# Output projection of a hybrid attention layer: the last two groups of weights as 2 x 2 blocks with seven products, and a fixed order on DVE and ACT behind the last attention slot

## The chip, the cores and the metric

One Trainium2 chip, one of its cores. The metric is the device time of the whole kernel in microseconds (us). The engines are named as in the profile: PE is TensorE (matmuls; PEld are its weight loads), DVE is VectorE, ACT is ScalarE, POOL is GpSimd, SP is SyncE, which here only issues transfers. Each engine has a queue of its own and works through it in order.

## What is computed

A decoder layer of 512 tokens by 1024 channels in float32. A modulated RMSNorm and an input projection give queries, keys, values and gates for two groups of eight heads; group A does sliding-window attention, group B three branches of attention; each group's output is multiplied by a SiLU gate, and the two are joined and projected:

```python
y = jnp.concatenate([o_a.reshape(Bn, S, D_A) * jax.nn.silu(z_a.astype(jnp.float32)),
                     o_b.reshape(Bn, S, D_B) * jax.nn.silu(z_b.astype(jnp.float32))], axis=-1)
out = y.astype(x.dtype) @ w_out
return x + gate[:, None, :] * out
```

`w_out` is 1024 x 1024. This last product, with the gate and the sum behind it, is the part that the change touches.

## The kernel before

**Numbers as pairs.** Each float32 operand of a large matmul is kept as two tiles of type float32r: a high part, which ACT copies, and a low part, which DVE makes by subtracting the high part. A product takes three matmuls: high by high, high by low, low by high. For weights, `split` (from L166) does this for a piece of 128 x 512 elements: ACT at L176 writes `wh`, DVE at L177 writes `wl`. The pieces lie in a pool of four buffers each (`pw`); a fifth piece waits until the matmuls of the first are done. `split_to` (L182) calls `split` along a fixed list of weight groups up to a given piece plus `ahead` further ones. `load_next` (L150) issues the next raw weight load on SP (L158) when a raw buffer (`rawp`, five of them) is used up; two halves make one group.

**Layout of the output projection.** Everything is transposed: tokens lie along the free dimension. y consists of eight tiles of 128 channels x 512 tokens, `yh[c]` and `yl[c]`: c = 0 to 3 belong to group A, c = 4 to 7 to group B (r = c - 4). `make_y` (L805) forms y from the attention output and the gate (DVE, L808), its high part (ACT, L810) and its low part (DVE, L811). The weights come in four groups o0 to o3, each for 256 of the 1024 outputs. `unit_col` (L478) does one channel group of 128 outputs: eight steps k, each three matmuls (L484) of 128 x 128 weights by 512 columns, into one PSUM bank `pj`; `PJ` hands out three banks in turn. Behind it DVE computes gate times bank plus x (L1037, tile `fin`) and SP stores the result (L1038). x comes by a load on ACT's queue (L1025 for the first two channel groups, L1031 for the others). The eighth channel group is done in two halves of 256 tokens.

**Where the order comes from.** The attention is a row of slots (`run`): scores on PE, softmax on DVE and ACT, scaling on DVE (`slot_scale`, L907), transposes on PE copied by ACT (`slot_trans`, tile `ptT`, L923 and L933), and the products with V on PE (`slot_pv`, L949 and L955, bank `po`). Projection work is fed between the slots as a stream. The instructions are then placed on each engine's queue by a list scheduler of the programming framework, which takes what it holds to be ready and urgent; PE's instructions of the attention blocks are chained in the written order with `in_order` (L66) through `block` (L490), and the two early loads of x are placed with it on ACT's queue. Nothing chains DVE and ACT in the output projection. When the last slot's `slot_pv` is done, y7 is made straight from PSUM; y4 and y5 had been kept as plain attention outputs (`ob`, L964) because their gates weren't ready at their time, and are made at the end of the program too; y6 had been made earlier.

Of the kernel before, what the change touches and what calls it, by code (L numbers as in the profile page):

```python
# [9 lines left out]
F32 = mybir.dt.float32  # L10
# [4 lines left out]
OP = mybir.AluOpType  # L15
# [10 lines left out]
LINE = 640  # L26
GW = 280
AHEAD = 6
NT2 = 40
WAIT_L, WAIT_M = 4, (0, 8)  # L30
PER_A, PER_B = 3.6, (3.5, 1.6, 7)
NEAR = 256
# [32 lines left out]
@contextmanager  # L65
def in_order(tc, after=(), only=None):  # L66

    traced = tc.nc.cur_bb.bb.instructions
    n = len(traced)
    last = dict(after)  # L70
    yield last
    info = mybir.DependencyInfo(mybir.DependencyClass.NoSync, mybir.DependencyReason.DATA)
    for i in tc.nc.cur_bb.bb.instructions[n:]:
        if only and i.engine != only:
            continue
        if i.engine in last:
            tc.add_manual_dep(i, last[i.engine].name, info, reason="in_order")
        last[i.engine] = i
# [3 lines left out]
def hybrid_layer_kernel(ctx, tc, A, out):  # L82
# [67 lines left out]
    def load_next():  # L150
        if pending:
            g, h = pending.pop(0)
            t = rawp.tile([128, 4, GW], F32, name="raw")
            if g[:4] == "gate":
                raws[g, h] = t.rearrange("p a b -> p (a b)")[:, 0:D]
            else:
                raws[g, h] = t[:, :, 0:A["w_" + g].shape[3]]
            SP.dma_start(raws[g, h], A["w_" + g][h])  # L158

    COL = ("kv_cmp", "z_a0", "z_a1", "z_b0", "z_b1", "o0", "o1", "o2", "o3")  # L160
    split_list = [(g, p) for g in ("kv_cmp", "kv_sel", "kv_win_g", "q_b0", "q_b1", "z_a0", "z_a1", "z_b0", "z_b1",
                                   "o0", "o1", "o2", "o3") for p in range(4)]
    split_pos = {e: n for n, e in enumerate(split_list)}
    split_done = [0]

    def split(g, p):  # L166

        if g in COL:
            src = raws[g, p % 2][:, :, 128 * (p // 2):128 * (p // 2) + 128]
        else:  # L170
            src = raws[g, p // 2][:, 2 * (p % 2):2 * (p % 2) + 2, :]
        sh = [src.shape[1], src.shape[2]]
        view = lambda t: t[:, 0:sh[0] * sh[1]].rearrange("p (k n) -> p k n", k=sh[0])
        wh = view(pw.tile([128, 2 * GW], F32R, name="wh"))
        wl = view(pw.tile([128, 2 * GW], F32R, name="wl"))
        ACT.activation(wh, src, AF.Copy)  # L176
        DVE.tensor_tensor(wl, src, wh.bitcast(F32), op=OP.subtract)  # L177
        pieces[g, p] = (wh, wl)
        if p == 3 or (p == (2 if g in COL else 1)):
            load_next()  # L180

    def split_to(g, p, ahead):  # L182

        while split_done[0] < min(len(split_list), split_pos[g, p] + ahead + 1):
            n, q = split_list[split_done[0]]
            if not all((n, h) in raws for h in ((0, 1) if n in COL else (q // 2,))):
                break
            split(n, q)
            split_done[0] += 1
# [242 lines left out]
    def W2(name, shape=(128, 512)):  # L432
        return mp.tile(list(shape), F32, name=name, tag="w2", bufs=5)
# [41 lines left out]
                              start=k == 0 and m == 0, stop=k == 7 and m == 2)  # L475
                yield cost

    def unit_col(g, ch, bank, src=(hh, hl), tok=slice(0, S)):  # L478

        for k in range(8):  # L480
            split_to(g, 2 * ch + k // 4, AHEAD)
            wh, wl = (x[:, k % 4, :] for x in pieces[g, 2 * ch + k // 4])
            for m, (w, h) in enumerate(((wh, src[0][k]), (wh, src[1][k]), (wl, src[0][k]))):
                PE.matmul(bank, w, h[:, tok], start=k == 0 and m == 0, stop=k == 7 and m == 2)  # L484
            yield 0.65

    chain = {}
# [1 line left out]
    @contextmanager  # L489
    def block():  # L490

        with in_order(tc, chain, PE.engine) as last:
            yield
        chain.update(last)

# [304 lines left out]
        else:  # L800
            sz[n - 4] = z

    yh, yl = {}, {}

    def make_y(c, o, z):  # L805

        yf = W2("yf")
        DVE.scalar_tensor_tensor(yf, o, 0.5, z, op0=OP.mult, op1=OP.mult)  # L808
        yh[c], yl[c] = T2(F32R, f"yh{c}"), T2(F32R, f"yl{c}")
        ACT.activation(yh[c], yf, AF.Copy)  # L810
        DVE.tensor_tensor(yl[c], yf, yh[c].bitcast(F32), op=OP.subtract)  # L811

    def gen2():
        posts.append(cmp_attn())
# [122 lines left out]
    def slot_pv(sl):  # L937
        kind, r, br, i = sl["id"]
        if (kind, r) not in po:
            po[kind, r] = ps_o.tile([128, 512], F32, name="po")  # L940
        o = po[kind, r]
        v = (va, vs, vw, None)[br]
        nb, j0 = sl["w"] // 128, sl["lo"] // 128
        last = kind == "a"
        first_of = kind == "a" or br == 3
        for b in range(nb):
            for g in range(2):
                vb = (vs, vw)[b][:, 0] if br == 3 else v[:, j0 + b]
                PE.matmul(o[64 * g:64 * g + 64, 128 * i:128 * i + 128], vb[:, 64 * g:64 * g + 64],  # L949
                          sl["T"][g][:, b, :], start=first_of and b == 0, stop=last and b == nb - 1,  # L950
                          skip_group_check=True)
        if i == NB - 1 and br in (0, 2):
            if kind == "b":
                for e in range(2):
                    PE.matmul(o, vc[e].rearrange("p g d -> p (g d)"), PTc[r], start=False, stop=e == 1,  # L955
                              skip_group_check=True)
            if kind == "a":
                o_a[r] = T2(F32, f"oa{r}")
                ACT.activation(o_a[r], o, AF.Copy)
            elif r in sz:  # L960
                make_y(4 + r, o, sz[r])
            else:
                o_a["b", r] = T2(F32, f"ob{r}")
                ACT.activation(o_a["b", r], o, AF.Copy)  # L964

    late = {}

    def run(slots, stream):
        n = len(slots)
        group = []  # L970
        for t in range(n + 3):
            per = PER_A if t < 16 else PER_B[t - 16 >= PER_B[2]]
            if t < n:
                kind, r, br, i = slots[t]["id"]
                if kind == "a" and i == 0 and r >= 2:
                    load_bias_b(r - 2)
            if 0 <= t - 2 < n:
                with block():
                    slot_trans(slots[t - 2])
            if 0 <= t - 1 < n:  # L980
                slot_scale(slots[t - 1])
            if t < n:
                with block():
                    slot_scores(slots[t])
                if t == n - 12:
                    late[ACT.engine] = [i for i in tc.nc.cur_bb.bb.instructions if i.engine == ACT.engine][-1]
            stream.adv(per / 2)
            if 0 <= t - 3 < n:
                group.append(slots[t - 3])
                kind, r, br, i = slots[t - 3]["id"]  # L990
                if i == NB - 1:
                    with block():
                        for sl in group:
                            slot_pv(sl)
# [21 lines left out]
    for r in range(4):  # L1016
        if 4 + r not in yh:
            make_y(4 + r, o_a["b", r], sz[r])


    with in_order(tc, late, ACT.engine):
        xrs = []
        for n in range(2):
            xrs.append(mp.tile([128, S], F32, name="xr", tag="qc", bufs=2))
            ACT.dma_start(xrs[n], A["xT"][n])  # L1025
    for n in range(8):
        if n < 2:
            xr = xrs[n]
        else:
            xr = mp.tile([128, S], F32, name="xr", tag="qc", bufs=2)  # L1030
            ACT.dma_start(xr, A["xT"][n])  # L1031
        f = W2("fin")
        for tok in ((slice(0, S),) if n < 7 else (slice(0, 256), slice(256, S))):
            b = PJ()[:, tok]
            for _ in unit_col(f"o{n // 2}", n % 2, b, (yh, yl), tok):
                pass
            DVE.scalar_tensor_tensor(f[:, tok], b, gate[:, n:n + 1], xr[:, tok], op0=OP.mult, op1=OP.add)  # L1037
            SP.dma_start(out[n][:, tok], f[:, tok])  # L1038


def _layout(inp):
# [24 lines left out]
    rows = np.concatenate([pair(r) for r in range(4)] + [512 + pair(r) for r in range(4)])  # L1066
    wo = g("w_out")[0][rows].reshape(8, 128, 4, 256)
    for q in range(4):
        a[f"w_o{q}"] = halves(wo[:, :, q].transpose(1, 0, 2))
# [41 lines left out]
```

## Time and profile before

| | |
|---|---|
| three runs | 311.12, 312.45, 313.27 us; median 312.45 |
| profiled execution, its own time | 312.03 us |
| its span, first to last instruction | 309.4 us |
| mean granted TensorE clock | 0.999 |
| DVE busy over the span | 241.6 us (78%) |
| ACT busy over the span | 194.9 us (63%) |
| last matmul ends, last DVE instruction ends | 306.25, 306.76 us |

A span is counted from the first instruction of the core to its last, the landing of the last store included; the execution's own time is 2.6 us longer. Rows of groups give the line of the kernel, the engine, the operation with the tile that it writes and those that it reads, the shape, the count, then busy time and mean duration in ns, and the engine's idle time ahead of them. Rows of the timeline give start and length in us; a row with a count is a run of equal instructions, and its length goes from the first start to the last end. Instructions of one engine overlap a little, so the distance of two starts is shorter than a duration.

### The profile page before, as it was taken

Reading aid. Unit: us, or ns where it says so; the run is one execution under the profiler, and the core shown is the slowest. Engines: PE = TensorE matmul, PEld = TensorE weight load, DVE = VectorE, ACT = ScalarE, POOL = GpSimd, SP = SyncE. Lnnn points to the kernel's source line nnn. Section 1 sums busy time; section 2 is a strip of 40 time slices with the busy share of each in tenths; the row PEclk is TensorE's granted clock in tenths of the full one; section 3 lists DMA queues with packets and bytes.
Section 4 is the critical chain, followed back from the end, with each engine's and each line's share of the span. In section 5 each row is a group of like instructions: output and inputs, shape, how many; then the busy total and the mean of one; then the engine's idle time right before and its main releaser. Section 6 shows DMA issues by size and latency. Waiting matters only on the chain.

```text
span 309.4 us, 5849 instructions
## 1 busy us (share of the span) xinstructions
PE 302.0 (98%) x2119; PEld 255.2 (82%) x2119; DVE 241.6 (78%) x666; ACT 194.9 (63%) x472; POOL 4.1 (1%) x22
## 2 busy tenths in 40 slices
PE   8999999999999999999999999999999999999995
PEld 3678888788988999889887888888888888788885
DVE  5679998999967567898999999988789696544221
ACT  5686448668967675676936665869778877422000
POOL 0000000000000000000000000000000000000000
PEclk9999999999999999999999999999999999999999
DMA  7999969800390909170454004140420220254101
GB/s 252 382 407 408 406 202 251 307 0 0 117 328 13 293 4 263 45 271 2 154 182 158 20 2 138 65 138 3 136 71 0 68 70 2 68 172 135 68 34 68
DMA packets 28231, 44.11 MB, mean 143 GB/s; under 512 B 1787, under 2 KB 19612, under 8 KB 28204
## 3 DMA queue, kind: packets, MB, share of 16 engines
q1 hardware_dynamic: 26908, 41.57, 39.3%
q10 hardware_dynamic: 1296, 2.18, 2.3%
q8 instruction: 16, 0.26, 0.3%
q14 instruction: 11, 0.09, 0.1%
HBM read 41.61 MB, written 2.14 MB: 141 GB/s over the span
## 4 chain that ended last, share of the span: by engine, by line
PE 78%; DVE 11%; ACT 4%; DMA 3%; issue 1%; SPq 1%; DVEq 0%; ACTq 0%
PE pj L484 28%; PE po L949 8%; PE sq L292 8%; PE pj L474 8%; PE s L874 7%; PE pt L932 4%; PE skv L293 4%; PE pt L922 3%; PE s L603 3%; DVE qs L535 2%; DMA raw<-in_w_gate 2%; DVE raw L709 2%; DMA xTp<-in_xT 2%; DVE wl L177 1%; PE s L666 1%
## 5 line engine op out<-in xcount | busy, mean ns | idle before, releaser
L176 ACT ACTIVATE wh<-raw 128x512 fp32r<-128x512 f32 (+1 forms) x52 | 31.3, 635 | 18.0 <-PE pj L484 14.1
L474 PE MATMUL pj<-wl,hh 128*128 128x256 f32 (+1 forms) x128 | 36.8, 288 | 0.1
L474 PE MATMUL pj<-wh,hh 128*128 128x256 f32 (+1 forms) x128 | 37.0, 289 | 0.0
L474 PE MATMUL pj<-wh,hl 128*128 128x256 f32 (+1 forms) x128 | 36.5, 285 | 0.0
L177 DVE TENSOR_TENSOR wl<-raw,wh 128x512 fp32r<-128x512 f32 (+1 forms) x52 | 34.9, 690 | 1.8 <-ACT wh L176 1.7
L886 ACT ACTIVATE pp<-pp,nm 128x256 f32<-128x256 f32 (+2 forms) x48 | 29.3, 615 | 7.0 <-DVE nm L879 6.9
L484 PE MATMUL pj<-hl,wh 128*128 128x512 f32 x80 | 32.2, 402 | 0.0
L484 PE MATMUL pj<-hh,wl 128*128 128x512 f32 x80 | 32.0, 400 | 0.0
L484 PE MATMUL pj<-hh,wh 128*128 128x512 f32 x80 | 32.0, 400 | 0.0
L879 DVE CUSTOM_DVE_ANT_0 pp<-s,bias 128x256 f32<-128x256 f32 (+2 forms) x48 | 25.6, 553 | 4.1 <-PE s L874 3.6
L484 PE MATMUL pj<-yh,wl 128*128 128x512 f32 (+1 forms) x72 | 26.6, 370 | 0.0
L484 PE MATMUL pj<-yl,wh 128*128 128x512 f32 (+1 forms) x72 | 26.6, 369 | 0.0
L1037 DVE SCALAR_TENSOR_TENSOR fin<-pj,gate,xr 128x512 f32<-128x512 f32 (+1 forms) x9 | 6.2, 692 | 25.9 <-PE pj L484 25.9
L484 PE MATMUL pj<-yh,wh 128*128 128x512 f32 (+1 forms) x72 | 26.4, 371 | 0.0
L474 PEld LDWEIGHTS pj<-wl,hh 128*128 128x128 f32 x128 | 24.1, 188 | 0.6 <-DVE wl L177 0.3
L874 PE MATMUL s<-kTb,qs 128*128 128x256 f32 (+2 forms) x96 | 24.3, 356 | 0.0
L474 PEld LDWEIGHTS pj<-wh,hl 128*128 128x128 f32 x128 | 24.1, 188 | 0.2 <-issue 0.2
L474 PEld LDWEIGHTS pj<-wh,hh 128*128 128x128 f32 x128 | 24.1, 189 | 0.1
L907 DVE TENSOR_SCALAR pp<-pp,rr,grev 128x256 f32<-128x256 f32 (+2 forms) x48 | 21.0, 475 | 0.5
L933 ACT COPY ptT<-pt 128x384 f32<-128x384 f32 (+1 forms) x32 | 15.8, 528 | 6.0 <-PE pt L932 5.9
L534 ACT ACTIVATE qs<-pt 64x512 fp32r<-64x512 f32 x16 | 9.5, 592 | 13.4 <-PE pt L529 7.3
L484 PEld LDWEIGHTS pj<-hh,wh 128*128 128x128 f32 x80 | 15.1, 188 | 3.0 <-issue 0.2
(238 smaller groups left out, 721.4 us busy)
## 6 DMA issues: line engine op xcount, KB each, us to landing
ada_ring<-in_w_ada_rows SPq DMA_DIRECT2D x12, 512.0 KB, 7.2
raw<-in_w_cmp SPq DMA_DIRECT2D x8, 512.0 KB, 5.4
raw<-in_w_gate SPq DMA_DIRECT2D x8, 512.0 KB, 5.6
raw<-in_w_o SPq DMA_DIRECT2D x8, 512.0 KB, 4.2
wst_ring<-in_w_qkv_a SPq DMA_DIRECT2D x8, 384.0 KB, 7.7
xTp<-in_xT SPq DMA_DIRECT2D x8, 256.0 KB, 4.6
bias<-line_d SPq DMA_DIRECT2D x8, 256.0 KB, 4.1
raw<-in_w_q_b SPq DMA_DIRECT2D x4, 512.0 KB, 6.5
```

The lines of the kernel that those rows point to most:

```text
L176: ACT.activation(wh, src, AF.Copy)
L177: DVE.tensor_tensor(wl, src, wh.bitcast(F32), op=OP.subtract)
L292: PE.matmul(pj_q[tb], lt, w[:, 0:512], start=f, stop=l, skip_group_check=True)
L293: PE.matmul(pj_kv[tb // 2][:, tb % 2, :], lt, w[:, 512:768], start=f and tb % 2 == 0, stop=l, skip_group_check=True)
L474: PE.matmul(bank[:, t * n:(t + 1) * n], h[:, tb * 128:(tb + 1) * 128], w[:, k % 2, :], start=k == 0 and m == 0, stop=k == 7 and m == 2)
L484: PE.matmul(bank, w, h[:, tok], start=k == 0 and m == 0, stop=k == 7 and m == 2)
L874: PE.matmul(ps, qs[h][:, 128 * i:128 * i + 128], k[:, hl_, lo:lo + w], start=hl_ == 0, stop=hl_ == 1)
L879: DVE.tensor_tensor_reduce(out=P[:, g, 0:w], in0=ps, in1=bt, scale=1.0, scalar=init, op0=OP.add, op1=OP.min, accum_out=nm[:, g:g + 1])
L886: ACT.activation(P[:, g, 0:e], P[:, g, 0:e], AF.Exp, bias=nm[:, g:g + 1], scale=-1.0, accum_out=dn[:, g:g + 1])
L907: DVE.tensor_scalar(v, v, rr[:, g:g + 1], gates[:, g, br:br + 1], op0=OP.mult, op1=OP.mult)
L933: ACT.copy(T[:, 0:nb, :], rev(pt[:, 0:nb * 128].rearrange("p (b q) -> p b q", b=nb)))
L949: PE.matmul(o[64 * g:64 * g + 64, 128 * i:128 * i + 128], vb[:, 64 * g:64 * g + 64], sl["T"][g][:, b, :], start=first_of and b == 0, stop= ...
```

## The change

For the weight groups o2 and o3 the product of weights and y is seen as a product of 2 x 2 blocks: the 1024 input channels fall into group A and group B (512 each), the 256 outputs of a group into two of 128, and the 512 tokens into two of 256. The plain way takes eight block products; the change takes seven (a scheme of Strassen's kind in Winograd's form), of four y tiles each, so 4 x 3 = 12 matmuls of 128 x 128 weights by 256 columns. It needs

- four differences of weight blocks for each group (t1 to t4, DVE, 128 x 512) beside the blocks 11, 22 and 21; each of the seven gets a high and a low part of its own in a new pool (`pwo`, six buffers),
- four sums of y halves for each r (s1 to s4, DVE, 128 x 256), kept in pairs as s12 and s34, each pair with a high part (ACT) and a low part (DVE) of 128 x 512. They serve both groups,
- three PSUM banks for each group: r (products 1, 3, 5, 7 add up on it), v (products 2 and 4) and w (product 6). Behind each product DVE adds gate times the bank's present state to a half of `fin`; products 3, 4, 5 and 7 go on adding to a bank that DVE has read in between.

Groups o0 and o1 stay as they are, four units of `unit_col`, with `ahead` = 0. The plain y tiles `yf` move from a pool of five to the pool T2, which grows from 40 to 44. y7 no longer is made inside `slot_pv`. From the scaling of the last slot on, all DVE and ACT instructions of the output projection are chained in the written order, with `in_order`; ACT's loads of x are in that chain. PE's order isn't chained there. The last channel group is no longer split by a separate half loop. The host lays the weights of o2 and o3 out by blocks.

```diff
-NT2 = 40
+NT2 = 44
...
+    pwo = ctx.enter_context(tc.tile_pool(name="pwo", bufs=6))
+    ot = ctx.enter_context(tc.tile_pool(name="ot", bufs=3))
...
+    OUT = ("o2", "o3")
+    BLOCKS = ("11", "t1", "t2", "22", "t3", "21", "t4")
...
+    def split_out(g, p):
+
+        blocks = {f"{i + 1}{j + 1}": raws[g, i][:, 512 * j:512 * j + 512] for i in range(2) for j in range(2)}
+        wh, wl = (pwo.tile([128, 512], F32R, name=n) for n in ("woh", "wol"))
+        if p in blocks:
+            src = blocks[p]
+        else:
+            a, b = {"t1": ("12", "11"), "t2": ("22", "t1"), "t3": ("22", "12"), "t4": ("21", "t2")}[p]
+            sums = raws[g, "t"] = raws.get((g, "t"), {})
+            src = sums[p] = ot.tile([128, 512], F32, name="ot")
+            DVE.tensor_tensor(src, *({**blocks, **sums}[n] for n in (a, b)), op=OP.subtract)
+        ACT.activation(wh, src, AF.Copy)
+        DVE.tensor_tensor(wl, src, wh.bitcast(F32), op=OP.subtract)
+        pieces[g, p] = [t.rearrange("p (k n) -> p k n", k=4) for t in (wh, wl)]
+        if p in ("t3", "t4"):
+            load_next()
...
+    def high_low(src, names):
+
+        h, l = (T2(F32R, n) for n in names)
+        ACT.activation(h, src, AF.Copy)
+        DVE.tensor_tensor(l, src, h.bitcast(F32), op=OP.subtract)
+        return h, l
...
+    def y_sums(r, second):
+
+        (a0, a1), (b0, b1) = ([yf[c][:, t] for t in TOK] for c in (r, 4 + r))
+        if not second:
+            s12 = sums_y[r, 0] = T2(F32, "s12")
+            DVE.tensor_tensor(s12[:, TOK[0]], a1, b1, op=OP.add)
+            DVE.tensor_tensor(s12[:, TOK[1]], s12[:, TOK[0]], a0, op=OP.subtract)
+        else:
+            s34 = sums_y[r, 1] = T2(F32, "s34")
+            DVE.tensor_tensor(s34[:, TOK[1]], b0, sums_y[r, 0][:, TOK[1]], op=OP.subtract)
+            DVE.tensor_tensor(s34[:, TOK[0]], a0, a1, op=OP.subtract)
...
+    with in_order(tc, last, (DVE.engine, ACT.engine)):
...
+        early = [r for r in range(3) if 4 + r not in yh]
+        for r in early:
+            y_full(4 + r, o_a["b", r], sz[r])
+        for r in early:
+            y_split(4 + r)
+        for r in range(3):
+            y_sums(r, 0)
+        y_full(7, o_a["b", 3], sz[3])
+        y_sums_split(0, 0)
+        y_split(7)
+        y_sums_split(1, 0)
+        y_sums_split(2, 0)
+        y_sums(3, 0)
+        bank = [unit(0), unit(1)]
+        split_to("o1", 0, 0)
+        y_sums_split(3, 0)
+        final(0, bank[0], xrs[0])
+        split_to("o1", 1, 0)
+        y_sums(0, 1)
+        y_sums(1, 1)
+        final(1, bank[1], xrs[1])
+        xrs += [load_x(2), load_x(3)]
+        y_sums_split(0, 1)
+        split_to("o1", 3, 0)
+        bank += [unit(2), unit(3)]
+        y_sums_split(1, 1)
+        y_sums(2, 1)
+        split_to("o2", "11", 0)
+        y_sums(3, 1)
+        y_sums_split(2, 1)
+        final(2, bank[2], xrs[2])
+        split_to("o2", "t2", 0)
+        y_sums_split(3, 1)
+        split_to("o2", "t3", 0)
+        final(3, bank[3], xrs[3])
+
+        def out_product(g, bank, src, w, new):
+
+            wh, wl = pieces[g, w]
+            for r in range(4):
+                h, l = yp[src, r]
+                for m, (p, q) in enumerate(((wh, h), (wh, l), (wl, h))):
+                    PE.matmul(bank, p[:, r, :], q, start=new and r == 0 and m == 0, stop=r == 3 and m == 2,
+                              skip_group_check=True)
+
+        PRODUCTS = (("r", "11", "11", True, (0, 0, 0, False)), ("v", "s1", "t1", True, (1, 1, 0, False)),
+                    ("r", "s2", "t2", False, (1, 0, 0, False)), ("v", "s4", "22", False, (1, 0, 1, True)),
+                    ("r", "s3", "t3", False, (1, 1, 1, True)), ("w", "12", "21", True, (0, 0, 1, True)),
+                    ("r", "22", "t4", False, (0, 1, 0, True)))
+        todo = [(g, w) for g in OUT for w in BLOCKS][5:]
+        for q in range(2, 4):
+            g = OUT[q - 2]
+            xr, f = [], []
+            for n in (2 * q, 2 * q + 1):
+                xr.append(load_x(n))
+                f.append(W2("fin"))
+            part = {"r": PJ()[:, 0:256], "v": ps_s.tile([128, 512], F32, name="s")[:, 0:256], "w": PT()[:, 0:256]}
+            for p, src, w, new, (ch, t, more, done) in PRODUCTS:
+                out_product(g, part[p], src, w, new)
+                if todo:
+                    split_to(*todo.pop(0), 0)
+                n = 2 * q + ch
+                DVE.scalar_tensor_tensor(f[ch][:, TOK[t]], part[p], gate[:, n:n + 1], (xr, f)[more][ch][:, TOK[t]],
+                                         op0=OP.mult, op1=OP.add)
+                if done:
+                    SP.dma_start(out[n][:, TOK[t]], f[ch][:, TOK[t]])
```

More of the change, by code (lines that the diff above doesn't have):

```diff
@@ L73, in in_order @@
     for i in tc.nc.cur_bb.bb.instructions[n:]:
-        if only and i.engine != only:
+        if only and i.engine not in only:
             continue
@@ L155, in load_next @@
                 raws[g, h] = t.rearrange("p a b -> p (a b)")[:, 0:D]
+            elif g in OUT:
+                raws[g, h] = t.rearrange("p a b -> p (a b)")[:, 0:D]
             else:
@@ L158, in load_next @@
             SP.dma_start(raws[g, h], A["w_" + g][h])
-    COL = ("kv_cmp", "z_a0", "z_a1", "z_b0", "z_b1", "o0", "o1", "o2", "o3")
+    COL = ("kv_cmp", "z_a0", "z_a1", "z_b0", "z_b1", "o0", "o1")
+    OUT = ("o2", "o3")
+    BLOCKS = ("11", "t1", "t2", "22", "t3", "21", "t4")
     split_list = [(g, p) for g in ("kv_cmp", "kv_sel", "kv_win_g", "q_b0", "q_b1", "z_a0", "z_a1", "z_b0", "z_b1",
-                                   "o0", "o1", "o2", "o3") for p in range(4)]
+                                   "o0", "o1") for p in range(4)]
+    split_list += [(g, p) for g in OUT for p in BLOCKS]
     split_pos = {e: n for n, e in enumerate(split_list)}
     split_done = [0]
+    def split_out(g, p):
[13 more added lines that the diff above has]
+            load_next()
     def split(g, p):
+        if g in OUT:
+            split_out(g, p)
+            return
         if g in COL:
@@ L185, in split_to @@
             n, q = split_list[split_done[0]]
-            if not all((n, h) in raws for h in ((0, 1) if n in COL else (q // 2,))):
+            if not all((n, h) in raws for h in ((0, 1) if n in COL + OUT else (q // 2,))):
                 break
@@ L476, in unit_nat, with unit_col @@
                 yield cost
-    def unit_col(g, ch, bank, src=(hh, hl), tok=slice(0, S)):
+    def unit_col(g, ch, bank, src=(hh, hl), ahead=AHEAD):
         for k in range(8):
-            split_to(g, 2 * ch + k // 4, AHEAD)
+            split_to(g, 2 * ch + k // 4, ahead)
             wh, wl = (x[:, k % 4, :] for x in pieces[g, 2 * ch + k // 4])
             for m, (w, h) in enumerate(((wh, src[0][k]), (wh, src[1][k]), (wl, src[0][k]))):
-                PE.matmul(bank, w, h[:, tok], start=k == 0 and m == 0, stop=k == 7 and m == 2)
+                PE.matmul(bank, w, h, start=k == 0 and m == 0, stop=k == 7 and m == 2)
             yield 0.65
@@ L490, in block @@
     def block():
-        with in_order(tc, chain, PE.engine) as last:
+        with in_order(tc, chain, (PE.engine,)) as last:
             yield
@@ L801, in post_z, with y_full, y_split, y_sums_split @@
             sz[n - 4] = z
-    yh, yl = {}, {}
-    def make_y(c, o, z):
[L807 to L811, printed above, removed]
+    yf, yh, yl, yp, sums_y = {}, {}, {}, {}, {}
+    TOK = (slice(0, 256), slice(256, 512))
+    def high_low(src, names):
[3 more added lines that the diff above has]
+        return h, l
+    def y_full(c, o, z):
+        yf[c] = T2(F32, "yf")
+        DVE.scalar_tensor_tensor(yf[c], o, 0.5, z, op0=OP.mult, op1=OP.mult)
+    def y_split(c):
+        yh[c], yl[c] = high_low(yf[c], (f"yh{c}", f"yl{c}"))
+        if c >= 4:
+            r = c - 4
+            for n, d, e in (("11", r, 0), ("12", c, 0), ("22", c, 1)):
+                yp[n, r] = [x[d][:, TOK[e]] for x in (yh, yl)]
+    def make_y(c, o, z):
+        y_full(c, o, z)
+        y_split(c)
+    def y_sums(r, second):
[8 more added lines that the diff above has]
+            DVE.tensor_tensor(s34[:, TOK[0]], a0, a1, op=OP.subtract)
+    def y_sums_split(r, second):
+        t = high_low(sums_y[r, second], ("ysh", "ysl"))
+        for n, e in zip((("s1", "s2"), ("s3", "s4"))[second], TOK):
+            yp[n, r] = [x[:, e] for x in t]
     def gen2():
@@ L959, in slot_pv @@
                 ACT.activation(o_a[r], o, AF.Copy)
+            elif r == 3:
+                o_a["b", r] = o
             elif r in sz:
@@ L964, in slot_pv @@
                 ACT.activation(o_a["b", r], o, AF.Copy)
-    late = {}
+    late, last = {}, {}
     def run(slots, stream):
@@ L981, in run @@
                 slot_scale(slots[t - 1])
+                if t == n:
+                    for e in (DVE.engine, ACT.engine):
+                        last[e] = [i for i in tc.nc.cur_bb.bb.instructions if i.engine == e][-1]
             if t < n:
@@ L1015, in hybrid_layer_kernel @@
     stream.drain()
[L1016 to L1021, printed above, removed]
+    with in_order(tc, late, (ACT.engine,)):
         xrs = []
         for n in range(2):
-            xrs.append(mp.tile([128, S], F32, name="xr", tag="qc", bufs=2))
+            xrs.append(mp.tile([128, S], F32, name="xr", tag="qc", bufs=4))
             ACT.dma_start(xrs[n], A["xT"][n])
[L1026 to L1030, printed above, removed]
+    split_to("o0", 3, 0)
@@ L1031, in hybrid_layer_kernel, with final, load_x, unit @@
+    with in_order(tc, last, (DVE.engine, ACT.engine)):
+        def final(n, b, xr):
+            f = W2("fin")
+            DVE.scalar_tensor_tensor(f, b, gate[:, n:n + 1], xr, op0=OP.mult, op1=OP.add)
+            SP.dma_start(out[n], f)
+        def load_x(n):
+            xr = mp.tile([128, S], F32, name="xr", tag="qc", bufs=4)
             ACT.dma_start(xr, A["xT"][n])
[L1032 to L1035, printed above, removed]
-                pass
-            DVE.scalar_tensor_tensor(f[:, tok], b, gate[:, n:n + 1], xr[:, tok], op0=OP.mult, op1=OP.add)
-            SP.dma_start(out[n][:, tok], f[:, tok])
+            return xr
+        def unit(n):
+            b = PJ()
+            for _ in unit_col(f"o{n // 2}", n % 2, b, (yh, yl), 0):
+                pass
+            return b
+        early = [r for r in range(3) if 4 + r not in yh]
[41 more added lines that the diff above has]
+        PRODUCTS = (("r", "11", "11", True, (0, 0, 0, False)), ("v", "s1", "t1", True, (1, 1, 0, False)),
[3 rows of a table added]
+        todo = [(g, w) for g in OUT for w in BLOCKS][5:]
[15 more added lines that the diff above has]
+                    SP.dma_start(out[n][:, TOK[t]], f[ch][:, TOK[t]])
@@ L1068, in _layout @@
     for q in range(4):
-        a[f"w_o{q}"] = halves(wo[:, :, q].transpose(1, 0, 2))
+        a[f"w_o{q}"] = halves(wo[:, :, q].transpose(1, 0, 2)) if q < 2 else cc(
+            wo[:, :, q].reshape(2, 4, 128, 2, 128).transpose(0, 2, 3, 1, 4).reshape(2, 128, D))
     for n, name in enumerate(("w_cmp_k1", "w_cmp_v1")):
```

## The prediction

> **What bounds the kernel now.** I read the page first, then the chain of waits from 264 us on, then busy time by stretch over the same 42 us.
>
> ```profile
> span 309.4 us, 5849 instructions
> ...
> PE 302.0 (98%) x2119; PEld 255.2 (82%) x2119; DVE 241.6 (78%) x666; ACT 194.9 (63%) x472; POOL 4.1 (1%) x22
> ```
>
> ```profile
> 264.31 41.95 PE pj L484 x204
> 306.26 0.03 issue
> 306.28 0.48 DVE fin L1037
> ```
>
> ```profile
> core 0: us, PE busy (x) PEld busy (x) DVE busy (x) ACT busy (x) POOL busy (x), PEclk, DMA share, GB/s
> 264.15:273.00 8.85, 8.85 (x40) 7.11 (x39) 5.70 (x10) 4.10 (x8) 0.00 (x0) 1.00 0.26 90
> 273.00:284.00 11.00, 11.00 (x49) 8.88 (x48) 3.96 (x7) 3.33 (x6) 0.00 (x0) 1.00 0.53 168
> 284.00:295.00 11.00, 11.00 (x49) 8.91 (x48) 3.80 (x6) 0.63 (x1) 0.00 (x0) 1.00 0.19 72
> 295.00:306.80 11.80, 11.24 (x73) 9.96 (x71) 3.07 (x5) 0.00 (x0) 0.00 (x0) 1.00 0.15 56
> sum 42.65, PE 42.09 PEld 34.87 DVE 16.53 ACT 8.06 POOL 0.00; mean PE 10.52 PEld 8.72 DVE 4.13 ACT 2.02 POOL 0.00
> ```
>
> From 264.31 the end is one unbroken run of 204 matmuls of the output projection, and behind them one last combination on DVE. In these 42.65 us DVE is busy for 16.53. So TensorE sets the end, and whatever shortens its list is worth its full time, as long as DVE, which has some 26 us to spare, can feed it.
>
> **What the change takes from TensorE.** Two rows give the pitch of the narrow form, in which the last channel group is done now.
>
> ```profile
> 300.42 0.28 PE L484 MATMUL pj<-yh,wh 128*128 128x256 f32 x1
> ...
> 305.97 0.28 PE L484 MATMUL pj<-yh,wl 128*128 128x256 f32 x1
> ```
>
> The 48 matmuls of 256 columns start 5.55/47 = 0.118 us apart; the 156 of 512 columns before them (300.42 - 264.31)/156 = 0.2315. A product of the new form is 4 x 3 matmuls of 256 columns, 12 x 0.118 = 1.41 us. Eight for a block of 256 outputs is what is done now, seven is new; for two blocks that removes 2 x 1.41 = 2.8 us. After 264.31 TensorE has 84 x 0.2315 = 19.4 us of o0 and o1 (to about 283.8) and 14 x 1.41 = 19.8 us of products: it could end near 303.6.
>
> **What the change gives DVE.** Prices first. A row with a count shows the pitch (start to start), which is shorter than the duration.
>
> ```profile
> 259.48 1.00 DVE L907 TENSOR_SCALAR pp<-pp,rr,grev 128x512 f32<-128x512 f32 x2
> 260.40 0.69 DVE L177 TENSOR_TENSOR wl<-raw,wh 128x512 fp32r<-128x512 f32 x1
> 264.35 0.69 DVE L808 SCALAR_TENSOR_TENSOR yf<-po,szb 128x512 f32<-128x512 f32 x1 [3.26 <-PE po L955]
> 264.95 1.28 DVE L808 SCALAR_TENSOR_TENSOR yf<-ob,szb 128x512 f32<-128x512 f32 x2
> 266.15 1.89 DVE L811 TENSOR_TENSOR yl<-yf,yh 128x512 fp32r<-128x512 f32 x3
> ```
>
> ```profile
> L177 DVE TENSOR_TENSOR wl<-raw,wh 128x512 fp32r<-128x512 f32 x48 | 32.1, 686 | 1.8 <-ACT wh L176 1.7
> ...
> L1037 DVE SCALAR_TENSOR_TENSOR fin<-pj,gate,xr 128x512 f32<-128x512 f32 x7 | 5.3, 751 | 21.5 <-PE pj L484 21.5
> ...
> L671 DVE TENSOR_TENSOR pa<-pa,s 128x256 f32<-128x256 f32 x4 | 1.7, 414 | 0.0
> ...
> L1037 DVE SCALAR_TENSOR_TENSOR fin<-pj,gate,xr 128x256 f32<-128x256 f32 x2 | 1.0, 484 | 4.4 <-PE pj L484 4.4
> ```
>
> Two 512-wide operations take 266.15 - 264.95 = 1.20, so the pitch is 0.60 and the overlap 0.09. With 0.08 to 0.09 off, the others have pitches of 0.335 (two tensors, 256 wide), 0.40 (combination, 256 wide) and 0.67 (combination, 512 wide). The last slot's scaling leaves DVE at 260.40; from there the new list, in its fixed order, holds
>
> - 40 of 512: 3 yf, 3 yl, 8 low parts of y sums, 4 low parts for o1, 14 low parts for the blocks of o2 and o3, 8 weight differences (t1 to t4, twice): 24.0 us
> - 16 of 256 for the sums s1 to s4: 5.4 us
> - 4 combinations of 512 and 14 of 256: 2.7 + 5.6 us
>
> together 37.7 us against 17.2 now (16.53 and one L177 at 260.40). To end where DVE now starts its last combination it has 306.28 - 260.40 = 45.9 us, so 8.2 us of waiting would be free. The fixed order costs more. For each weight difference the program puts the DVE subtraction, ACT's high part and DVE's low part one behind the other; nothing else can stand between the two on DVE's queue.
>
> ```profile
> 247.98 0.69 DVE L808 SCALAR_TENSOR_TENSOR yf<-po,szb 128x512 f32<-128x512 f32 x1
> ...
> 248.70 0.64 ACT L810 ACTIVATE yh<-yf 128x512 fp32r<-128x512 f32 x1 [1.42 <-DVE yf L808]
> ...
> 249.37 0.69 DVE L811 TENSOR_TENSOR yl<-yf,yh 128x512 fp32r<-128x512 f32 x1 [0.31 <-ACT yh L810]
> ```
>
> This is the same chain for a y: DVE ends at 248.67, ACT runs from 248.70 to 249.34, DVE follows at 249.37: 0.03 us per handover. (Its first row and L907 between them show that DVE could then do something else; in the new order it can't.) A difference therefore holds DVE idle for 0.09 + 0.03 + 0.63 + 0.03 = 0.78 us, and the eight of them for 6.2 us. Where the source is ready earlier (blocks 11, 22, 21, o1, most y sums), ACT runs ahead and DVE doesn't wait.
>
> ```profile
> 261.19 1.07 ACT L933 COPY ptT<-pt 128x512 f32<-128x512 f32 x2 [0.19 <-PE pt L932]
> 265.13 1.17 ACT L810 ACTIVATE yh<-yf 128x512 fp32r<-128x512 f32 x2 [2.87 <-DVE yf L808]
> ```
>
> ```profile
> xr<-in_xT ACTq DMA_DIRECT2D x8, 256.0 KB, 2.6
> out_dram<-fin SPq DMA_DIRECT2D x7, 256.0 KB, 2.0
> ```
>
> Four smaller waits. The high parts of the two early y come behind the last ptT copies (to about 262.2), so DVE has nothing from 261.6 to 262.8: 1.2 us. In s1, s12 and s4, s34 the second reads the first: 8 x 0.11 = 0.9, and other handovers 0.35. The x of channel groups 4, 5 and 6, 7 are fetched from ACT's queue behind the high part of t3 (about 287.5 and 301.0), 2.6 us to landing, and the first combination of each block reads them: 0.7 + 1.0 us.
>
> **How they meet.** Laid out in order with these prices: unit 2 ends near 278.3 but DVE gets to its combination at 280.4; then come t1, t2, a y sum's low part, 22, t3, the combination of unit 3 and 21, so the first combination of o2 stands at 290.1. TensorE is through with unit 3 at 283.8, with products 1 and 2 at 286.7, and must stop: product 3 accumulates on the bank that this combination has yet to read. From here DVE leads. In the o2 loop it has 3 x 0.60 + 4 x 1.98 (t4 and the next t1, t2, t3) + 7 x 0.40 = 12.5 us for 7 x 1.41 = 9.9 us of products; it finds time for the second combination of o3 only at 306.0. TensorE then still has products 4, 5 and 7 of o3 to do (the sixth was brought forward into a stop), from 306.5, and DVE waits for them 1.3 + 1.0 + 1.3 = 3.65 us. DVE's stretch: 37.65 + 6.25 + 1.2 + 0.9 + 0.35 + 1.7 + 3.65 = 51.7, and 0.1 to the end of the last instruction: 260.40 + 51.8 = 312.2. Before, it was 306.76. So +5.4 us: 312.03 us for the profiled execution becomes **317.4 us** (its span 309.4 becomes 314.8). The profiled execution lies 0.4 below the median of the runs, 312.45.
>
> **What the trace doesn't show.** Handover at every step: 0.03 as above, or 265.13 - 265.04 = 0.09 as for the first yh of the tail, which makes 314.1 of 312.2; I take 0.03, seen twice. Order on TensorE isn't fixed by the change: if groups run strictly as written, it waits for y7 inside unit 0 and ends at 313.3; I take the interleaving that the trace of before has. x landings between 1.0 and the 4.2 us of the slowest xr would move the end by -1.6 to +3.2; I take the median 2.6. All else that moves costs nothing by the same layout: the o2 and o3 loads are issued well ahead of their use, the four new T2 buffers replace the yf that move there, and the 12 matmuls of unit 0 done before 264 stay there. If DVE's pitches fell to 0.55 the end would be 310.6. This gives 315.2 to 320.5 for this case.
>
> **Rivals.**
> *DVE keeps up, not slower.* It decides at product 3 of o2: the first combination would have to be done by 286.7 instead of 290.6, and later a difference would have to cost DVE 1.2 us rather than 1.98 (3 x 0.60 + 4 x 1.20 + 2.8 = 9.4, under 9.9). That would need the fixed order not to hold DVE between the two halves. Then only the 2.8 us count: 309.2. For it: 26 us of idle DVE. Against it: 37.7 us of work by measured pitches.
> *The small waits vanish.* The x land in time (-1.7) and the early high parts slip between the ptT copies (-1.2): 314.5.
> *A cold TensorE.* It now never stops; in the layout it stops for 2.9 us at 286.7 and 2.6 at 300.2.
>
> ```profile
> 308.50:309.00 0.50, 0.00 (x0) 0.00 (x0) 0.00 (x0) 0.00 (x0) 0.00 (x0) 1.00 0.00 0
> 309.00:309.40 0.40, 0.00 (x0) 0.00 (x0) 0.00 (x0) 0.00 (x0) 0.00 (x0) 0.52 0.00 0
> ```
>
> ```profile
> 1.22 4.50 PE L317 MATMUL skv<-zero 128*128 128x512 bf16 x11 [1.22 <-DVE wst_ring L300]
> ```
>
> The granted clock halves 2.75 us after the last matmul, and the first eleven matmuls of the kernel run at 0.41 us for 512 columns, 4.5 us long. If the second stop trips this, 4.5 us at half rate lose 2.25: 319.7. The Trainium skill (TensorE: Matmul & The Clock Gate, "What's actually happening") says that the clock is halved after an idle window of about 3.4 us on a clock that runs freely; by it neither stop is long enough for certain, and the sum stays at 317.4. The row above, at 2.75 us, speaks for a trip at either stop.
> *Stores hold the halves.* If a combination into one half of a fin tile waits until the other half is stored (2.0 us), twice on the last path: 321.4.
>
> **How the numbers follow.** DVE as the bound 0.58, small waits vanish 0.18, cold TensorE 0.12, stores 0.06, DVE keeps up 0.06. A measurement of this kernel can tell about 1% from no change, 3.1 us: slower means over 315.6. Slower: 0.54 of the 0.58, with 0.12 and 0.06, 0.72. Faster: 0.04 of the last. The rest, 0.24, is within 1%. The range runs from 313.0 (below it the last rival and a part of the small waits, about 0.1) to 320.5 (above it the stores and a part of the cold clock, about 0.1).
>
> **What would show it.** Right: DVE over 80% busy from 260 to 306 and 37 to 39 us there; gaps of 0.7 to 0.8 us on DVE ahead of each low part of a difference; TensorE stopped at about 286.7 for 2 to 4 us, released by DVE's combination; 14 products of 1.41 us. Wrong: no stop of TensorE between 284 and 300; a last product before 305; DVE pitches under 0.5 us for 512; low parts that follow without a gap.

## The result, and the profile after the change

The changed kernel takes 316.29 us (median of six runs, 315.61 to 317.49), the kernel before 311.71 (six runs, 311.02 to 313.27): a ratio of 1.0147, with a 95% interval of 1.0114 to 1.018. The profiled execution took 317.05 us, its span is 315.3; the forecast was 317.4 and 314.8. (Two experiments below, e2 and e4, have profiles from disturbed executions, so only their times are used.)

First the page of the changed kernel: its span, and the busy time of each engine.

```profile
span 315.3 us, 5998 instructions
...
PE 303.5 (96%) x2166; PEld 258.0 (82%) x2167; DVE 262.7 (83%) x713; ACT 202.9 (64%) x486; POOL 4.2 (1%) x22
```

DVE has 21 us more than before over the whole span, TensorE 1.5 more. Now the stretch from the end of the last slot's scaling on DVE to the end of the last combination, by windows; the columns are those that the prediction shows. Before and after, one fence for each:

```profile
260.40:306.76 46.36, 45.84 (x252) 38.12 (x250) 17.21 (x28) 9.74 (x18) 0.00 (x0) 1.00 0.26 88
```

```profile
260.75:312.47 51.72, 47.29 (x301) 41.02 (x299) 39.35 (x75) 18.33 (x33) 0.00 (x0) 0.97 0.23 80
284.00:290.00 6.00, 3.71 (x28) 3.26 (x26) 4.54 (x8) 2.93 (x5) 0.00 (x0) 1.00 0.22 58
290.00:296.00 6.00, 5.65 (x31) 5.22 (x32) 4.46 (x9) 1.78 (x3) 0.00 (x0) 0.72 0.19 73
```

The stretch grew by 51.72 - 46.36 = 5.36 us. In it TensorE is idle for 4.4 us (0.5 before), 2.3 of them between 284 and 290. The clock column shows 0.72 from 290 to 296; whether that costs anything is what e8 asks. Between kernels this stretch is the measure to use, because the point at which the attention ends differs from profile to profile (259.6 to 260.8 in all but one of those used here). The profile of the changed kernel, for one, has a mean clock of 0.97 in its first 50 us, where the others have 1.00; e8, the same kernel up to the output projection, begins the stretch at 259.62, 1.1 us earlier than the changed kernel.

The chain that ended last, where before there was one run of 204 matmuls on TensorE (start, length, engine and line):

```profile
281.80 0.61 DVE ot L183
282.43 0.64 ACT woh L184
283.09 0.69 DVE wol L185
...
287.04 0.61 DVE ot L183
287.69 2.63 DMA xr<-in_xT
290.44 0.48 DVE fin L1173
...
300.06 0.61 DVE ot L183
300.70 2.78 DMA xr<-in_xT
303.57 0.50 DVE fin L1173
304.11 1.70 PE pj L1153 x12
```

The end now goes through DVE and ACT: difference, high part, low part, one behind the other; from 281.80 to 303.57 no matmul is in it. The two DMA pieces are x loads that ACT could issue only behind a high part.

The same place on DVE's own timeline: length, and in brackets the idle time ahead of an instruction and what ended it.

```profile
281.71 0.68 DVE L183 TENSOR_TENSOR ot<-raw 128x512 f32<-128x512 f32 x1
283.09 0.69 DVE L185 TENSOR_TENSOR wol<-ot,woh 128x512 fp32r<-128x512 f32 x1 [0.70 <-ACT woh L184]
283.70 0.69 DVE L183 TENSOR_TENSOR ot<-raw,ot 128x512 f32<-128x512 f32 x1
285.14 0.69 DVE L185 TENSOR_TENSOR wol<-ot,woh 128x512 fp32r<-128x512 f32 x1 [0.76 <-ACT woh L184]
...
289.61 0.68 DVE L185 TENSOR_TENSOR wol<-raw,woh 128x512 fp32r<-128x512 f32 x1
290.44 0.48 DVE L1173 SCALAR_TENSOR_TENSOR fin<-pj,gate,xr 128x256 f32<-128x256 f32 x1
```

And TensorE beside it, from its last product that needs no combination on:

```profile
284.21 0.28 PE L1153 MATMUL pj<-yh,woh 128*128 128x256 f32 x1
...
285.62 0.28 PE L1153 MATMUL s<-ysh,woh 128*128 128x256 f32 x1
...
286.93 0.28 PE L1153 MATMUL s<-ysh,wol 128*128 128x256 f32 x1
289.24 0.39 PE L1153 MATMUL pt<-yh,woh 128*128 128x256 f32 x1 [2.03 <-ACT woh L184]
...
290.35 0.39 PE L1153 MATMUL pt<-yh,wol 128*128 128x256 f32 x1 [0.61 <-DVE wol L185]
...
290.98 0.38 PE L1153 MATMUL pj<-ysh,woh 128*128 128x256 f32 x1
```

Product 1 starts at 284.21 and product 2 at 285.62, 1.41 us later. Product 2 is through at 287.2, and then TensorE stops for 2.03 us. What ends the stop is the weights of block 21, for product 6 (tile `pt`), which runs ahead into the gap as far as it can; product 3 (tile `pj` again, with `ysh`) starts at 290.98, right behind the combination that began on DVE at 290.44.

### The profile page after: what moved, and what is told of

Same layout as the page of the kernel before. It is cut to its first block, busy times and chain, and to the rows that moved or that the text cites. A ratio compares the mean times of both kernels' runs of the same rounds, so it can differ in the third digit from the quotient of the medians.

```text
span 315.3 us, 5998 instructions
## 1 busy us (share of the span) xinstructions
PE 303.5 (96%) x2166; PEld 258.0 (82%) x2167; DVE 262.7 (83%) x713; ACT 202.9 (64%) x486; POOL 4.2 (1%) x22
## 4 chain that ended last, share of the span: by engine, by line
PE 70%; DVE 17%; DMA 5%; ACT 4%; issue 2%; SPq 1%; POOL 0%; DVEq 0%; ACTq 0%; POOLq 0%
PE pj L511 19%; PE sq L319 8%; PE s L936 7%; PE pj L501 7%; PE po L1011 7%; PE pt L994 4%; PE pt L984 4%; PE skv L320 4%; PE s L630 3%; DMA xr<-in_xT 2%; DVE wol L185 2%; DMA raw<-in_w_gate 2%; DVE qs L562 2%; PE pj L1153 2%; DMA xTp<-in_xT 2%
## 5 line engine op out<-in xcount | busy, mean ns | idle before, releaser
L204 DVE TENSOR_TENSOR wl<-raw,wh 128x512 fp32r<-128x512 f32 (+1 forms) x44 | 29.6, 690 | 1.9 <-ACT wh L203 1.7
L203 ACT ACTIVATE wh<-raw 128x512 fp32r<-128x512 f32 (+1 forms) x44 | 26.7, 638 | 0.4 <-PE pj L511 0.3
L941 DVE CUSTOM_DVE_ANT_0 pa<-s,bias,nsink 128x256 f32<-128x256 f32 (+1 forms) x32 | 14.3, 448 | 4.0 <-POOL pa L945 2.3
L511 PEld LDWEIGHTS pj<-hh,wl 128*128 128x128 f32 x80 | 15.1, 189 | 2.9
L511 PEld LDWEIGHTS pj<-hl,wh 128*128 128x128 f32 x80 | 15.0, 188 | 2.8 <-issue 0.2
L948 ACT ACTIVATE pa<-pa,nm 128x257 f32<-128x257 f32 (+1 forms) x32 | 15.3, 479 | 2.5 <-DVE nm L941 1.9
```

What stands on the lines that cost most here:

```text
L511: PE.matmul(bank, w, h, start=k == 0 and m == 0, stop=k == 7 and m == 2)
L941: DVE.tensor_tensor_reduce(out=P[:, g, 0:w], in0=ps, in1=bt, scale=1.0, scalar=init, op0=OP.add, op1=OP.min, accum_out=nm[:, g:g + 1])
L948: ACT.activation(P[:, g, 0:e], P[:, g, 0:e], AF.Exp, bias=nm[:, g:g + 1], scale=-1.0, accum_out=dn[:, g:g + 1])
```

## The experiments

The theory: the eight places where the fixed order puts difference, high part and low part side by side cost 0.78 us each on DVE, 6.2 us, and turn DVE into the bound. The rivals: the order alone costs it (whatever the products), DVE's added work costs it, the late x loads, or the halved clock. "Stretch" below always runs from the end of the last slot's scaling to the end of the last combination. Every ratio is to the kernel before.

**e1: the differences one step earlier.** A difference is subtracted ahead of the low part of the previous difference, so that something stands between it and its own low part. `diff_out` holds the subtraction of before and makes each difference once. Nothing is added or left out.

```diff
+        src = diff_out(g, p)
+        if p[0] == "t":
+            later = [e for e in split_list[split_pos[g, p] + 1:] if e[1][0] == "t"]
+            if later:
+                diff_out(*later[0])
```

Expected: 

> Same instructions as the changed kernel; only each weight difference is subtracted on DVE one step earlier, ahead of the low part of the difference before it, so that ACT copies while DVE works. If DVE's fixed list with its eight waits of 0.7 us sets the end (my theory), about 5.3 us come back: 311 us, ratio to the kernel before 0.995 to 1.005. If TensorE's products, its half clock in the stop near 291.5 to 294.8 or the x loads are the cost, no more than 1 us comes back: 315 to 316.

Measured: 309.82 us, 0.997 (0.9929 to 1.001). DVE and the stretch of e1:

```profile
280.62 0.68 DVE L182 TENSOR_TENSOR ot<-raw 128x512 f32<-128x512 f32 x1
281.33 0.69 DVE L182 TENSOR_TENSOR ot<-raw,ot 128x512 f32<-128x512 f32 x1
282.00 0.69 DVE L194 TENSOR_TENSOR wol<-ot,woh 128x512 fp32r<-128x512 f32 x1
282.61 0.68 DVE L182 TENSOR_TENSOR ot<-raw 128x512 f32<-128x512 f32 x1
283.21 0.68 DVE L194 TENSOR_TENSOR wol<-ot,woh 128x512 fp32r<-128x512 f32 x1
```

```profile
259.65:305.05 45.40, 44.13 (x301) 39.23 (x299) 38.79 (x75) 18.20 (x33) 0.00 (x0) 1.00 0.26 91
```

The same 75 instructions on DVE, and no idle time between the halves of a difference. The stretch falls from 51.72 to 45.40, by 6.3 us: the whole loss and 1 us more, a little beyond the 5.3 us expected. Its chain goes through DVE up to 287.61 and from there through TensorE to the end. The theory holds: with the same instructions in another order the loss is gone. The 6.3 is close to eight times 0.78, but it doesn't measure these waits alone: TensorE sets the end of e1, and the waits for x are gone from it as well.

**e2: no fixed order.** The chain of DVE and ACT is taken out, all else stays.

```diff
-    with in_order(tc, last, (DVE.engine, ACT.engine)):
+    if True:
```

Expected: 

> Same instructions as the changed kernel, but DVE and ACT are not chained in the output projection; the framework's scheduler places them. Theory (the amount of DVE work is nearly affordable, the waits of the fixed order are the loss): the scheduler can fill the waits, 310 to 313 us. Rival (the amount of DVE work is too much in any order): 315 us or more.

Measured: 310.02 us, 0.9966 (0.9934 to 0.9998). The list scheduler's own order loses nothing either, so it is the order and not the list of instructions that makes the changed kernel slower.

**e3: the fixed order with eight products.** The matmuls and weight splits of before, but with DVE and ACT chained behind the last slot.

```diff
-    COL = ("kv_cmp", "z_a0", "z_a1", "z_b0", "z_b1", "o0", "o1")
-    OUT = ("o2", "o3")
+    COL = ("kv_cmp", "z_a0", "z_a1", "z_b0", "z_b1", "o0", "o1", "o2", "o3")
+    OUT = ()
...
```

Expected: 

> Eight products, as before the change, but DVE and ACT chained in the written order and with the changed pools for y. Theory: the chain alone costs nothing, since DVE has little to do: 311 to 312.5 us, within 0.3% of the kernel before. Rival (the fixed order itself, or the moved y tiles, are the loss): 314 us or more.

Measured: 311.05 us, 0.9993 (0.9956 to 1.0031), in the range expected; stretch 46.49 against 46.36. A fixed order by itself is free here, where DVE has only 17.4 us of work in the stretch and no difference to wait for.

**e4 and e9: the differences on POOL.** DVE loses eight instructions and no longer waits inside a difference. e4 keeps the pool of three `ot` tiles, e9 has eight.

```diff
-            DVE.tensor_tensor(src, *({**blocks, **sums}[n] for n in (a, b)), op=OP.subtract)
+            POOL.tensor_tensor(sums[p], *({**blocks, **sums}[n] for n in (a, b)), op=OP.subtract)
...
-    ot = ctx.enter_context(tc.tile_pool(name="ot", bufs=3))
+    ot = ctx.enter_context(tc.tile_pool(name="ot", bufs=8))
```

Expected of e4: 

> The changed kernel with the eight weight differences subtracted on POOL instead of DVE (4.8 us less on DVE, and no wait behind them if POOL is ahead). Theory: DVE falls below TensorE's list, which then ends the kernel: 308 to 310 us, ratio 0.988 to 0.996, if POOL takes under 2 us for one difference (the trace has no such row); with 4 us each the differences of o2 come late and it ends near 315. Rival (TensorE or its clock is the cost): 315 to 316.

Expected of e9: 

> The run with the differences on POOL, with eight buffers for them instead of three, so that POOL needn't wait until DVE is done with the first difference (it stood 28 us with three). If the late start was the loss there, all eight are ready before 285 and it ends at 308.5 to 310 us. If the two engines hold each other up (in that run DVE took 1.55 us for a low part while POOL subtracted, against 0.68 else), the same slowing falls between 250 and 285 instead, on DVE operations of the attention and of y: 4 to 8 POOL operations of 1.3 to 1.7 us slow DVE by up to 0.9 us each, 311 to 314 us.

Measured: e4 315.36 us, 1.013 (1.0085 to 1.0176): a miss, hardly better than the change. e9 313.82 us, 1.0038 (0.9987 to 1.0089), in the second of the ranges expected. By the code of e4 the first three differences fill the three buffers, and the fourth can't start before DVE has made the low part of t1. With eight buffers the output projection itself is cured: its stretch is 46.05 us, and TensorE waits for `fin` once, 1.8 us. But the stretch begins at 262.52, 1.8 us later than in the changed kernel and 2.9 later than in e8. Not all eight differences came early, either: five were done by 257.2, and the last three ran from 282.32 to 287.39. POOL and DVE of e9, then DVE's low parts of weights from 240 to 285 us, and behind them the same group in the changed kernel:

```profile
247.63 1.30 POOL L182 TENSOR_TENSOR ot<-raw,ot 128x512 f32<-128x512 f32 x1 [29.52 <-DMA raw<-in_w_o]
...
285.65 1.74 POOL L182 TENSOR_TENSOR ot<-raw,ot 128x512 f32<-128x512 f32 x1
```

```profile
286.16 1.78 DVE L842 TENSOR_TENSOR ysl<-s,ysh 128x512 fp32r<-128x512 f32 x1
```

```profile
L209 DVE TENSOR_TENSOR wl<-raw,wh 128x512 fp32r<-128x512 f32 x6 | 5.1, 866 | 0.1
```

```profile
L204 DVE TENSOR_TENSOR wl<-raw,wh 128x512 fp32r<-128x512 f32 x6 | 4.0, 685 | 0.1
```

While POOL subtracts (285.65 to 287.39), a DVE instruction that takes 0.68 us elsewhere takes 1.78 and ends 0.55 us behind it. So DVE pays for the difference anyway, where the two overlap. Ahead of the stretch, between 249 and 253 us, two low parts took 1.47 and 1.77 us beside POOL, 1.9 us more together than they take alone. Whether this is what ends the attention later in e9, or whether its engine order also came out another way, stays open.

**e6: no differences and no sums.** The eight weight differences and the sixteen sums of y halves are left out; their places are taken by plain blocks and plain y tiles, so this kernel computes something else, with all matmuls, splits and combinations in place.

```diff
-            src = sums[p] = ot.tile([128, 512], F32, name="ot")
-            DVE.tensor_tensor(src, *({**blocks, **sums}[n] for n in (a, b)), op=OP.subtract)
+            src = sums[p] = blocks[a]
...
+        sums_y[r, second] = yf[4 * second + r]
```

Expected: 

> Leaves out all 8 weight differences and all 16 sums of y halves: the high and low parts are made straight from blocks and y tiles, everything else is as in the changed kernel (14 products of 12 matmuls, the same order). DVE loses 8 x 0.60 + 16 x 0.34 = 10.2 us of work and the eight waits. Theory: TensorE is the bound and the seventh product's saving shows in full: 2.8 us under the kernel before, 308.6 us, ratio 0.991. Rival (the product form costs TensorE more than 1.41 us for each product, or the bank order stops it anyway): 311 us or more.

Measured: 309.26 us, 0.9923 (0.9882 to 0.9964). Its stretch, and the chain that ended last from 263 us on:

```profile
259.68:303.67 43.99, 43.47 (x301) 39.05 (x299) 29.18 (x51) 16.92 (x33) 0.00 (x0) 1.00 0.28 94
```

```profile
263.59 19.67 PE pj L510 x85
283.26 1.41 PE pj L1144 x12
284.67 1.41 PE s L1144 x12
...
301.74 1.43 PE pj L1144 x12
...
303.19 0.48 DVE fin L1164
```

TensorE is never held: fourteen products of 1.41 to 1.44 us without a gap. This is what seven products for eight are worth when DVE keeps up, 46.36 - 43.99 = 2.4 us of the 2.8 that the pitch promised. It also checks the prices on DVE: 24 instructions less take 39.35 - 29.18 = 10.2 us out of its busy time, and 8 x 0.60 + 16 x 0.335 is 10.2.

**e7: x earlier.** The x tiles of channel groups 4 and 5 are loaded with those of 2 and 3, and those of 6 and 7 just ahead of the loop over o2 and o3, not inside it.

```diff
-        xrs += [load_x(2), load_x(3)]
+        xrs += [load_x(n) for n in range(2, 6)]
...
+        xrs += [load_x(6), load_x(7)]
...
-                xr.append(load_x(n))
+                xr.append(xrs[n])
```

Expected: 

> The changed kernel with the x of channel groups 4 to 7 fetched one or two combinations earlier; nothing else. Theory: DVE waits 0.2 and 0.6 us for them in the profile of the changed kernel, on the path: 315.2 to 315.7 us, 0.6 to 1.1 under the changed kernel. Rival (the transfers are a main part of the loss): 313 or less. Rival (hidden anyway): 316 or more.

Measured: 315.53 us, 1.0126 (1.0105 to 1.0148). Its stretch:

```profile
259.76:310.79 51.03, 46.26 (x301) 40.72 (x299) 39.27 (x75) 18.26 (x33) 0.00 (x0) 0.97 0.25 80
```

It is 51.03 us, 0.7 less than in the changed kernel. The two waits for x were 0.23 and 0.61 us by DVE's pitches (290.44 and 303.57 against the end of the list before them), 0.84 together, so nearly all of them comes back. A small wait, not the cause.

**e8: TensorE kept warm.** Eighteen more matmuls behind product 2 of each block, into the bank that product 6 starts afresh, fill TensorE's stops.

```diff
+                if src == "s1":
+                    for e in range(18):
+                        PE.matmul(part["w"], pieces[g, "11"][0][:, e % 4, :], yp["11", e % 4][0], start=True, stop=True,
+                                  skip_group_check=True)
```

Expected: 

> The changed kernel with 18 further matmuls of 256 columns (2.1 us) on the bank of product 6 behind product 2 of each block, in time in which TensorE would stop; product 6 clears that bank later. Theory: the clock stays whole near 291 to 295, but the time doesn't move by more than 0.8 us (315.5 to 317), since DVE leads there. Rival (the half clock is on the path: 14 matmuls at 0.21 instead of 0.12 us): 1.3 us or more come back, 315 us or less.

Measured: 317.1 us, 1.0191 (1.0142 to 1.0241), 0.1 us above the range expected; its four runs go from 315.94 to 320.41, and the profiled one is the lowest. Windows of e8:

```profile
259.62:311.33 51.71, 49.48 (x337) 43.70 (x335) 39.36 (x75) 18.36 (x33) 0.00 (x0) 1.00 0.23 80
291.00:295.00 4.00, 4.00 (x36) 4.00 (x35) 3.09 (x6) 1.33 (x3) 0.00 (x0) 1.00 0.00 0
```

The clock stays at 1.00 throughout the stretch, which is 51.71 us long against 51.72. The half clock of the changed kernel lies in time in which TensorE would have waited for DVE anyway. That rival falls.

**e5: the cure of e1 and three more steps.** e1, with the x of e7, t1 and t2 of o2 subtracted while DVE waits for the two early high parts, and the split of block 21 behind the first combination of o2.

```diff
+        for p in ("t1", "t2"):
+            diff_out("o2", p)
...
-        todo = [(g, w) for g in OUT for w in BLOCKS][5:]
+        todo = [None] + [(g, w) for g in OUT for w in BLOCKS][5:]
...
```

Expected: 

> As the run with the early subtractions, and besides: t1 and t2 of o2 are subtracted in DVE's wait for the first high parts (1.35 us idle near 262), the x of channel groups 4 to 7 are fetched one or two combinations earlier, and the low part of block 21 comes behind the first combination of o2. Theory: what is left of TensorE's stop near 287 (0.8 us in the run with the early subtractions) goes, TensorE is the only bound: 308.5 to 309.3 us, ratio 0.991 to 0.994. Rival (something else than DVE holds the end): 309.8 or more, as without these steps.

Measured: 309.16 us, 0.9926 (0.9903 to 0.9948), faster than the kernel before and than the changed one.

```profile
260.07:304.48 44.41, 43.90 (x301) 39.17 (x299) 38.97 (x75) 18.05 (x33) 0.00 (x0) 1.00 0.28 93
```

DVE does the same 39 us of work in 44.41 us, and TensorE is idle for 0.5. It is 0.4 us from e6, in which the sums cost nothing at all: with the order right, DVE's extra 22 us are nearly hidden. What each of the three further steps brought was not taken apart.

## Why the prediction was right, point by point

- *The bound moves from TensorE to DVE.* Right: the chain above. TensorE was through with unit 3 at 284.2 (forecast 283.8), stopped from 287.2 (286.7), the first combination of o2 began at 290.4 (290.1), the second combination of o3 at 305.97 (306.0), and the last instruction ended at 312.47 (312.2) from a start 0.35 later.
- *DVE's list, 37.7 us by pitch.* Right: 74 instructions, and the 75th of the window is the tail of the scaling; e6 bears out the pitches. DVE was to be over 80% busy from 260 to 306 with 37 to 39 us:

```profile
260.00:306.00 46.00, 42.76 (x267) 37.05 (x268) 37.42 (x71) 18.61 (x33) 0.00 (x0) 0.96 0.24 81
```

- *Eight waits of 0.78 us, 6.2 us.* Right, and the decisive term. The waits of the changed kernel from 260 us on (engine and line that wait, for what; us, times, longest):

```profile
DVE wol L185 <- ACT woh L184: 5.7, 8, 0.8
...
DVE fin L1173 <- PE pj L1153: 2.4, 2, 1.5
...
DVE fin L1173 <- PE s L1153: 1.4, 1, 1.4
...
DVE fin L1173 <- DMA xr<-in_xT: 0.5, 1, 0.5
```

  Eight times 0.70 to 0.76 of idle time and 0.08 of overlap lost; by start to start 283.09 - 281.71 = 1.38, less the pitch of 0.60, is 0.78. A handover cost 0.04 and 0.02 us there (DVE ends at 282.39, ACT runs from 282.43 to 283.07, DVE follows at 283.09), so the 0.03 was the right choice and not the 0.09. (The 314.1 given for 0.09 can't be followed from the rows: eight times two handovers of 0.06 more are 1.0 us, not 1.9.) Taking the waits away (e1) gave back the whole loss.
- *Smaller waits.* Three of four were off, in opposite directions. The early high parts held DVE for 1.35 us (forecast 1.2). The other handovers came to 0.96 (forecast 0.35): 0.78 at 272.83, at a sum whose low part follows at once, and 0.18 at 268.84, at the low part of y7. In the sums only the pair s1, s2 has a second instruction that reads the first, while s3 and s4 are independent; the forecast misread the code. Between the first such pair stood the low part of a weight, so three pairs waited, 0.11 to 0.12 each: 0.35 us, not 0.9. The x loads cost 0.84 us, not 1.7: they landed 2.63 and 2.78 us behind their issue, near the 2.6 of the forecast, but DVE itself came to them later. (For the 1.0 us that the forecast took as the quickest landing of an x, the kernel before has no row: its quickest took 2.5.)
- *Final waits of DVE on TensorE, 3.65 us.* 2.4 + 1.4 by the waits, 4.0 with the lost overlap. Summed up with these sizes the terms give 37.65 + 6.25 + 1.35 + 0.96 + 0.35 + 0.84 + 4.0 = 51.4 of the 51.72 measured; 0.3 us lies in lost overlaps that were not followed one by one. That the forecast of 51.7 is met to 0.02 us is luck: the errors of its smaller terms cancel.
- *Two stops of TensorE, 2.9 and 2.6 us.* The first was 2.03 + 0.61, with product 3 behind the combination as forecast. But the combination didn't end the 2.03 us, as the signs of a right forecast had it: the high part of block 21 did, for product 6. Nor did all 14 products take 1.41 us: at the halved clock product 3 of o2 took 2.38 us, from 290.98 to the start of product 4 at 293.36. The second came apart: product 2 of o3 was done in pieces around product 7 of o2, and from 302 to 304.2 TensorE is idle for 0.6 us in all, in gaps of up to 0.3.
- *The rivals.* "DVE keeps up" needed a difference to cost 1.2 us in place of 1.98, which is what e1 and e5 make of it; as the change is written it doesn't. Of the 2.9 us of "Small waits vanish" the x part shrank by 0.9, while the early high parts stayed; e7 shows what is left of the x part at 0.7. "A cold TensorE" did happen, behind the first stop and not the second, and not on the path (e8). For "stores hold the halves" no wait on a store stands among the combinations.

The median of 316.29 lies 1.1 us below the forecast, which was made for the profiled execution: that one came out at 317.05, 0.35 under it. This closeness is luck in part too. Its span came out 0.5 us over the forecast, and the time outside the span was 1.75 us (317.05 - 315.3) in place of the 2.6 carried over from before. By medians the change costs 316.29 - 311.71 = 4.6 us where 5.4 was forecast; by the stretch, which the forecast was added up for, it costs 5.36.

## What to carry to other kernels

When a fixed order is written by hand, read it as each engine's own queue: a chain engine A, engine B, engine A with nothing between the two halves on A cost A the whole of B's instruction and two handovers here, all eight times. One step of lookahead (make the next input before finishing the present one) removed it at no cost in instructions. By work alone DVE still had 45.9 - 37.7 = 8.2 us to spare after the change; the waits ahead of the last combinations (6.25 + 1.35 + 0.96 + 0.35 + 0.84 = 9.75 us) took more than that. So count the waits that an order creates as well as the work that it holds.

## What was not expected of the hardware

*The clock halves behind two stops in close succession.* Windows of the changed kernel; the figure behind POOL's is the granted clock:

```profile
291.50:291.60 0.10, 0.10 (x3) 0.10 (x3) 0.02 (x1) 0.04 (x1) 0.00 (x0) 0.91 0.00 0
291.60:291.80 0.20, 0.20 (x3) 0.20 (x3) 0.00 (x0) 0.20 (x1) 0.00 (x0) 0.50 0.00 0
...
294.90:295.00 0.10, 0.10 (x2) 0.10 (x2) 0.00 (x0) 0.07 (x1) 0.00 (x0) 0.53 0.00 0
```

The clock is halved from about 291.6 to 295.0, for 3.4 us, although TensorE had been at work again from 290.35 on and its longest stop was 2.03 us (287.2 to 289.24). The prediction had looked for a trip at a single long stop; here it fell behind two stops with two recorded matmuls (289.24 and 289.46) between them. With the stops filled (e8) it stayed at 1.00, which speaks for the stops as the cause; which of the two, and after how long, no run shows. The Trainium skill (TensorE: Matmul & The Clock Gate, "What's actually happening") gives an idle window of about 3.4 us that runs freely: the length of the half-clock time agrees, but no idle stretch of that length stands ahead of it.

*DVE and POOL hold each other up on two-input instructions.* 0.68 us became 1.78 in e9 beside a POOL subtraction, and that took 1.74 us beside DVE against 1.30 at 247.63. Both of the slowed low parts near 250 us ended like this one, 0.55 to 0.56 us behind POOL's subtraction. The Trainium skill (SBUF — State Buffer, "SBUF: two separate sides") says that a DVE instruction with two SBUF inputs and a GpSimd one that reads SBUF lock each other out, whichever starts first keeping the other waiting for its whole length; these rows agree.
